# Eighteen of a layer's 22 tail gates by seven products a pair, in a two-layer decoder trunk

## The chip, the cores and the metric

The kernel runs on one core of one Trainium2 chip. The metric is device time in microseconds (us); lower is better. Matmuls run on TensorE (PE; its weight loads are listed apart as PEld), elementwise work on VectorE (DVE), ScalarE (ACT) and GpSimd (POOL), and DMAs are issued by SyncE (its queue is SPq). Each engine works through its instructions in a fixed order: one that waits holds up all that stand behind it on that engine, and this holds for the DMA issues of SyncE too.

## What is computed

Two layers, each of four token mixers whose results are merged under sigmoid gates (cut from the reference):

```
h = rms_norm(x, norm_g)
z = h @ w_in                    # 1024 tokens, 1024 channels; the last 4096 columns are merge_logits
...
gates = sigmoid(merge_logits + b_merge).reshape(bsz, seq, 4, 1024)
merged = (gates[:, :, 0] * (y_a @ w_br_a) + gates[:, :, 1] * (y_b @ w_br_b)
          + gates[:, :, 2] * (y_c @ w_br_c) + gates[:, :, 3] * (y_m @ w_br_m))
x = x + merged @ w_out
```

The kernel calls the branches i = 0, 1, 2, 3 (a, b, c, m) and cuts each branch's gate into 8 blocks c of 128 channels, so a layer has 32 gates (i, c). A gate is a 1024x1024 by 1024x128 product, a scale per token, and a tanh.

## The kernel before

Everything is kept with channels on the 128 partitions and the 1024 tokens along the row. For precision every operand is split into a high part in fp32r and a low part (`xh`, `xl`, `wh`, `wl`), and a product is the three matmuls high by high, low by high, high by low (`block_into`). A 128x1024 result takes two matmuls of 512 columns for each; one gate (8 blocks of input channels) is 48 matmuls, and a branch's projection `y @ w_br` for one c is 12 matmuls (24 for i = 1).

`wsplit` loads a weight tile (`wr`, two buffers), casts it on DVE (`wh`) and subtracts on POOL (`wl`). `cmn` multiplies the product by `rsb`, the per-token scale, on DVE, out of PSUM. The PSUM tiles of these products, `mm`, have two buffers of 128x1024. A Tile scheduler decides each engine's order from the order of the code and from priorities, and it puts in the waits; the buffers of the pools (38 row tiles from `U`, two each of `wr`, `wh`, `wl`) decide when a load may start.

Ten gates of a layer (the list `BG`: all of i = 1, and (3, 6) and (3, 7)) are made earlier, by `background`, and stored in DRAM as `bgscr`. The other 22 are made in the tail of the layer, after `branch_a`: `merge` runs for i = 0, 2, 3, 1, and for each c makes the gate with `cmn` and a tanh on ACT, then the projection `psy`, then `(1 + gate) * psy` on DVE (L103), and adds it to `merged` on POOL. For a gate of `BG` it loads the tile `gate` from `bgscr` in place of the product. `gated` fetches the branch outputs from DRAM (`ysscr`) while the merge before is running. After the merges come eight blocks of the output projection `w_out`.

Of the kernel before, what the change touches and what calls it, by code (L numbers as in the profile page):

```python
# [35 lines left out]
BR_OFF = (0, 2, 6, 8)  # L36
# [8 lines left out]
class Trunk:  # L45
# [174 lines left out]
    def setup(self):  # L220
        nc, a, L = self.nc, self.a, self.L
        C = self.C
        self.ident = C([P, P], "ident")
        make_identity(nc, self.ident)
        self.identb = C([P, P], "identb", BF16)
        make_identity(nc, self.identb)
        self.ones = C([P, 1], "ones")
        nc.vector.memset(self.ones, 1.0)
        self.onesr = C([P, P], "onesr", F32R)
        nc.vector.tensor_copy(self.onesr, self.ones.to_broadcast([P, P]))  # L230
        self.maskb = C([P, P], "maskb", BF16)
# [34 lines left out]
        self.bgscr = self.dp.tile([len(BG), P, S], F32, name="bgscr")  # L266
# [1019 lines left out]
    def bg_gate(self, l, br, b):  # L1286
        bi = {1: B_BG, 2: B_CG, 3: B_MG}[br] + b
        y = {1: self.ybscr, 2: self.gscr, 3: self.ymscr}[br][b]
        ri = {1: 0, 2: 0, 3: 4}[br] + b
        self.background(l, bi, y=y, ri=self.riscr[ri], dst=self.ysscr[BR_OFF[br] - 2 + b])  # L1290

    def bg_merge(self, l, i, c):
        at = l * 32 + 8 * i + c
        self.background(l, B_MRG + 8 * i + c, bias=self.bm_half[:, at:at + 1], dst=self.bgscr[BG.index((i, c))])

    def gated(self, br, own):

        ys = []
        for b in range(BR_KT[br]):
            pair = None  # L1300
            if b < min(own, 2):
                pair = self.wpair(True)
            elif b < own:
                pair = [self.fp.tile([P, S], F32R, tag="ft", name=self._n("ys")) if 2 * b + k < 7 else self.U("ys", F32R)
                        for k in range(2)]
            ys.append(self.fetch(self.ysscr[BR_OFF[br] - 2 + b], pair, self.wraw(True), self.nc.vector))
        return ys

    def silu2(self, l, bi):
# [94 lines left out]
            ya.append((hi, lo))  # L1404
        return ya

    def merge(self, l, i, ys, first=False, last=False, ahead=None):

        nc = self.nc
        kt = BR_KT[i]  # L1410
# [2 lines left out]
            self.mg = []  # L1413
        if last:
            self.mgs = []
        res = None

        def weights(c):
            off = (BR_OFF[i] * 8 + c * kt) * P
# [2 lines left out]

        nxt = weights(0)
        for c in range(8):
            if ahead and ahead[0] == c:
                res = ahead[1]()
# [23 lines left out]
        return res  # L1450

    def run(self):
        nc, a = self.nc, self.a
# [16 lines left out]
        for l in range(self.L):  # L1470
# [69 lines left out]


NU = 38
AH = (6, 4, 3)
NBW = 2
LOW = 100000

# [120 lines left out]
```

## Time and profile before

| | |
|---|---|
| time, median of 3 runs (lowest to highest) | 2438.87 us (2436.58 to 2439.66) |
| the profiled execution's own time | 2440.25 us |
| its span, first to last instruction | 2438.5 us |
| mean granted TensorE clock | 0.988 |
| PE busy | 2325.2 us, 95% of the span |
| PEld busy | 1855.2 us, 76% |
| DVE / POOL / ACT busy | 1215.9 / 775.0 / 706.5 us |
| HBM traffic | 97 GB/s over the span |

The busy times are sums over the whole program; PE and PEld run side by side. The tails with which this case deals lie at about 809 to 1130 us (layer 0) and 2104 to 2355 us (layer 1), and the output projections follow.

### The profile page before, as it was taken

The page shows a single profiled execution, that of the slowest core. Times are in us where ns is not written, and L with a number is a line of the kernel's source. Part 1 is how long each engine was busy: PE and PEld are TensorE (multiplying, and loading weights), DVE is VectorE, ACT ScalarE, POOL GpSimd, SP SyncE. Part 2 cuts the span into 40 slices and gives each one's busy share as a digit, 9 for nine tenths or more (in the row PEclk, how much of TensorE's full clock was granted, in tenths as well). Part 3 has the DMA queues.
Part 4 walks back from the last instruction along what each step waited for, and adds up shares of the span by engine and source line. Part 5 has one row for each costly group of instructions (what it writes and reads, how often), then busy time and mean ns, then how long its engine had stood idle before and what let it go on. Part 6 is the DMA issues. An engine that isn't in the chain of part 4 may idle for free. (4 is left out here: it accounts for less than half of the span.)

```text
span 2438.5 us, 28178 instructions
## 1 busy us (share of the span) xinstructions
PE 2325.2 (95%) x11174; PEld 1855.2 (76%) x11174; DVE 1215.9 (50%) x1871; ACT 706.5 (29%) x1233; POOL 775.0 (32%) x605
## 2 busy tenths in 40 slices
PE   7998889989999999999999888999999999999999
PEld 5766677867778888888877666787777888888887
DVE  6455784366676323236244556714666652233351
ACT  4121253247762101101111213522577420111010
POOL 3533113432304214342435421143322132244411
PEclk9999999999999999999999999999999999999999
DMA  4226343242332112222432363413423211122342
GB/s 153 75 93 184 115 138 102 82 123 79 95 106 66 61 44 70 69 77 105 156 100 73 96 188 108 139 49 103 125 83 109 80 44 52 56 92 79 103 156 69
DMA packets 91700, 237.56 MB, mean 97 GB/s; under 512 B 25200, under 2 KB 34352, under 8 KB 91568
## 3 DMA queue, kind: packets, MB, share of 16 engines
q1 hardware_dynamic: 91568, 235.76, 30.4%
q8 instruction: 88, 1.44, 0.2%
q14 instruction: 44, 0.36, 0.1%
HBM read 175.27 MB, written 60.46 MB: 97 GB/s over the span
## 5 line engine op out<-in xcount | busy, mean ns | idle before, releaser
L96 POOL TENSOR_TENSOR wl<-wr,wh 128x1024 fp32r<-128x1024 f32 (+3 forms) x125 | 295.9, 2367 | 946.1 <-DVE wh L152 634.7
L176 PE MATMUL mm<-xh,wh 128*128 128x512 f32 x1216 | 378.7, 392 | 9.1 <-ACT xh L106 8.7
L152 DVE CAST wh<-wr 128x1024 fp32r<-128x1024 f32 (+2 forms) x110 | 78.4, 713 | 618.6 <-PE mm L176 539.8
L176 PE MATMUL mm<-xh,wl 128*128 128x512 f32 x1216 | 376.1, 390 | 0.8 <-POOL wl L96 0.8
L176 PE MATMUL mm<-xl,wh 128*128 128x512 f32 x1216 | 376.8, 390 | 0.0
L176 PEld LDWEIGHTS mm<-xh,wh 128*128 128x128 f32 x1216 | 227.3, 188 | 59.9 <-ACT xh L106 8.7
L176 PEld LDWEIGHTS mm<-xh,wl 128*128 128x128 f32 x1216 | 228.3, 188 | 49.7 <-POOL wl L96 1.6
L176 PEld LDWEIGHTS mm<-xl,wh 128*128 128x128 f32 x1216 | 228.4, 188 | 49.0 <-issue 0.8
L176 PE MATMUL bg<-xh,bh 128*128 128x512 f32 x576 | 229.2, 416 | 15.5 <-DVE bgx L96 15.5
L176 PE MATMUL bg<-xl,bh 128*128 128x512 f32 x576 | 226.3, 411 | 0.0
L176 PE MATMUL bg<-xh,bl 128*128 128x512 f32 x576 | 224.1, 409 | 1.0 <-POOL bl L96 1.0
L96 POOL TENSOR_TENSOR bl<-br,bh 128x1024 fp32r<-128x1024 f32 x36 | 96.4, 2678 | 317.0 <-DVE bh L152 203.3
L106 ACT ACTIVATE cmn<-cmn,bmh 128x1024 f32<-128x1024 f32 x44 | 50.6, 1151 | 440.7 <-DVE cmn L96 440.7
L96 DVE TENSOR_TENSOR pT<-tr,pT 128x512 fp32r<-128x512 f32 x224 | 125.6, 571 | 42.8 <-ACT pT L106 42.1
L176 PEld LDWEIGHTS bg<-xh,bh 128*128 128x128 f32 x576 | 111.8, 195 | 46.0 <-DVE bgx L96 25.6
L176 PE MATMUL pv<-pT,v 128*128 128x512 f32 (+3 forms) x384 | 134.0, 388 | 7.9 <-DVE pT L96 5.1
L106 ACT ACTIVATE pT<-tr 128x512 fp32r<-128x512 f32 x224 | 111.0, 505 | 86.6 <-PE tr L1087 77.3
L176 PEld LDWEIGHTS bg<-xh,bl 128*128 128x128 f32 x576 | 111.1, 193 | 24.9 <-issue 3.2
L1054 DVE TENSOR_REDUCE mx<-mm 128x1 f32<-128x128 f32 (+7 forms) x128 | 96.5, 754 | 64.5 <-PE mm L176 63.7
L176 PEld LDWEIGHTS bg<-xl,bh 128*128 128x128 f32 x576 | 111.3, 194 | 21.8 <-issue 4.0
L106 ACT ACTIVATE pr<-mm,nm,qs 128x128 f32<-128x128 f32 (+7 forms) x128 | 106.3, 830 | 0.9
L1087 PE MATMUL tr<-ident,pr 128*128 128x128 f32 x576 | 97.9, 275 | 0.3 <-ACT pr L106 0.2
(449 smaller groups left out, 4173.7 us busy)
## 6 DMA issues: line engine op xcount, KB each, us to landing
wr<-in_w_cm_dram SPq DMA_DIRECT2D x76, 512.0 KB, 3.6
br<-in_w_cm_dram SPq DMA_DIRECT2D x36, 512.0 KB, 3.7
bgscr<-bgx SPq DMA_DIRECT2D x20, 512.0 KB, 3.1
gate<-bgscr SPq DMA_DIRECT2D x20, 512.0 KB, 5.6
ysscr<-bgx SPq DMA_DIRECT2D x16, 512.0 KB, 2.6
br<-ysscr SPq DMA_DIRECT2D x16, 512.0 KB, 3.4
wr<-in_w_out_dram SPq DMA_DIRECT2D x16, 512.0 KB, 3.7
bgr<-riscr SPq DMA_DIRECT2D x24, 256.0 KB, 4.8
```

The lines of the kernel that those rows point to most:

```text
L96: (eng or self.nc.vector).tensor_tensor(out=out, in0=x, in1=y, op=op)
L106: self.nc.scalar.activation(out, x, f, **k)
L152: self.nc.vector.tensor_copy(hi[:, :n], raw)
L176: self.nc.tensor.matmul(out, lhsT, rhs, start=start, stop=stop)
L1054: nc.vector.reduce_max(out=mx, in_=ps[:, 0:n], axis=AX.X)
L1087: nc.tensor.transpose(pt[:, k * P:(k + 1) * P], pts[k][:, st * P:(st + 1) * P], self.ident)
```

## The change

In `after` no gate is made inside `merge` any more. All 32 are stored in `bgscr` first, and `merge` loads each as a `gate` tile. The 22 tail gates are made ahead of the merges:

- Four, (0, 0) to (0, 3), in the ordinary way (`gate`: `cmn`, tanh, a store).
- Eighteen as nine pairs (i, c), (i, c + 1) by Strassen's scheme in its seven-product form: the weights of the two gates are the two rows of a 2x2 block matrix, the input channels are cut into halves (blocks k and k + 4), and the tokens into halves of 512. Each of the seven products has 4 blocks by 3 matmuls, so a pair takes 84 matmuls of 512 columns in place of 96. `pair_weights` forms the four sums of weights (DVE, tiles `sa`), and splits seven 128x512 weights (`sw`: high part on ACT, low part on POOL, two of the seven on DVE). `pairs` adds the products up on DVE (tiles `us`; the results go to `wh` and `wl` tiles), POOL multiplies by `rsb`, ACT takes the tanh, each on 512 columns, and SyncE stores the halves.
- The sums of x that the products need (`T` and `T4`, and later `xl`/`xh` written over) come from `x_sums`, for k = 0 to 3: it loads blocks k and k + 4 of x again (`xp`), scales them on ACT, forms four sums on POOL (`tp`, `t1`, in place), and splits three of them (ACT copy, DVE subtraction). The code interleaves these with the four ordinary gates. `x_sums2` then splits the fourth sum over half of `xg`.

Two smaller edits come with it. `gated` fetches through `U("yr")` in place of the `br` tile, all of them in the first two merges. The additions to `merged` alternate between POOL (odd c) and DVE. The last attention gate's `background` gets ordinary priority (`fore`).

```diff
+    def x_sums(self, l, src, k):
+        g, v = self.nc.gpsimd, self.nc.vector
...
+        b11, b12, b21, b22 = self.x_part(src, l, k)
+        t = self.U("tp")
+        t3, t2 = t[:, 0:512], t[:, 512:1024]
+        self.tt(t3, b22, b12, SUB, eng=g)
+        self.tt(t2, t3, b11, ADD, eng=g)
+        self.tt(self.t1[k // 2][:, k % 2 * 512:k % 2 * 512 + 512], b12, b11, SUB, eng=g)
+        self.tt(b21, b21, t2, SUB, eng=g)
+        self.split(*self.T[3][k], t3)
+        self.split(*self.T[2][k], t2)
+        self.split(*self.T[4][k], b21)
+    def pair_weights(self, aps):
+        raw = [self.wraw() for _ in range(2)]
...
+        self.tt(s1, a21, a22, ADD)
+        self.tt(s2, s1, a11, SUB)
+        self.tt(s3, a11, a21, SUB)
+        self.tt(s4, a12, s2, SUB)
+        for i, a in enumerate((a11, s2, s3, a12, s1, a22, s4)):
+            w = self.U("sw", F32R)
+            hi, lo = half(w)
+            self.split(hi, lo, a, sub_eng=self.nc.vector if i in (1, 4) else self.nc.gpsimd)
+            yield hi, lo
+    def pairs(self, todo):
...
+            q1, q2 = half(self.mm())
+            self.act(u1, prod(q1, 11), AF.Copy)
+            self.tt(u2, prod(q2, 2), u1, ADD)
+            q1, q2 = half(self.mm())
+            self.tt(u3, prod(q1, 3), u2, ADD)
+            finish(0, c1[0], prod(q2, 21), u1)
+            q1, q2 = half(self.mm())
+            p5 = prod(q1, 1)
+            self.tt(u4, p5, u2, ADD)
+            finish(1, c2[1], p5, u3)
+            finish(0, c2[0], prod(q2, 4), u3)
+            finish(1, c1[1], prod(self.pv(), 22), u4)
+            done(c1, c2)
+    def gate(self, l, i, c):
+        g, b = self.cmn(l, B_MRG + 8 * i + c), l * 32 + 8 * i + c
+        self.act(g, g, AF.Tanh, scale=0.5, bias=self.bm_half[:, b:b + 1])
+        self.nc.sync.dma_start(out=self.bgscr[8 * i + c], in_=g)
...
-            if (i, c) in BG:
-                g = self.U("gate")
-                nc.sync.dma_start(out=g, in_=self.bgscr[BG.index((i, c))])
-            else:
-                g = self.cmn(l, B_MRG + 8 * i + c)
-                self.act(g, g, AF.Tanh, scale=0.5, bias=self.bm_half[:, l * 32 + 8 * i + c:l * 32 + 8 * i + c + 1])
+            g = self.U("gate")
+            nc.sync.dma_start(out=g, in_=self.bgscr[8 * i + c])
...
-                self.tt(self.mg[c], self.mg[c], g, ADD, eng=None if last else nc.gpsimd)
+                self.tt(self.mg[c], self.mg[c], g, ADD, eng=nc.gpsimd if c % 2 and not last else None)
...
             ysa = self.branch_a(l)
-            ys = self.merge(l, 0, ysa, first=True, ahead=(AH[0], lambda: self.gated(2, 2)))
-            ys = self.merge(l, 2, ys, ahead=(AH[1], lambda: self.gated(3, 0)))
-            ys = self.merge(l, 3, ys, ahead=(AH[2], lambda: self.gated(1, 4)))
-            self.merge(l, 1, ys, last=True)
+            for k in range(4):
+                self.x_sums(l, src, k)
+                if k:
+                    self.gate(l, 0, k - 1)
+            self.gate(l, 0, 3)
+            self.x_sums2()
+            todo = [(i, c) for i in (0, 2, 3, 1) for c in range(8) if (i, c) not in BG][4:]
+            self.gate_pairs(l, todo[::2])
...
+            self.merge(l, 0, ysa, first=True, ahead={0: lambda: get(2, 0), 4: lambda: get(3, 0)})
+            self.merge(l, 2, ys[2], ahead={0: lambda: get(1, 4)})
+            self.merge(l, 3, ys[3])
+            self.merge(l, 1, ys[1], last=True)
```

**Where the instructions stand.** DVE in the tail of layer 0, before, from the end of `branch_a` on (`cmn_...<-mm_...,rsb` reads a gate's product out of PSUM, `merged` is the gated projection, a `wh` or `wkh` cast is the high part of the next weights):

```order
L96 TENSOR_TENSOR yal_1333_6772<-cmn_1308_6597,yah_1332_6771 128x1024
L152 CAST wkh_1335_6777<-wr_1334_6775 128x1024
L96 TENSOR_TENSOR wkl_1336_6778<-wr_1334_6775,wkh_1335_6777 128x1024
L96 TENSOR_TENSOR cmn_1337_6781<-mm_1341_6788,rsb_89_557 128x1024
L103 SCALAR_TENSOR_TENSOR merged0_1343_6852<-cmn_1337_6781,mm_1342_6839 128x1024
L152 CAST wh_1356_6936<-wr_1355_6934 128x1024
L152 CAST wh_1363_7009<-wr_1362_7007 128x1024
L96 TENSOR_TENSOR cmn_1344_6854<-mm_1348_6861,rsb_89_557 128x1024
```

The same place in `after` (`mm_1358`, `mm_1366`, `mm_1374`, `mm_1379` are the products of the four ordinary gates in this order; `tp_1350`, `tp_1353`, `tp_1361` and the `xp` tiles belong to k = 0, 1, 2):

```order
L96 TENSOR_TENSOR T4_1344_6785<-xp_1349_6792,T4_1342_6783 128x512
L152 CAST wh_1377_7037<-wr_1376_7035 128x1024
L96 TENSOR_TENSOR cmn_1354_6823<-mm_1358_6830,rsb_89_557 128x1024
L96 TENSOR_TENSOR T_1340_6781<-tp_1353_6812,T_1338_6779 128x512
L96 TENSOR_TENSOR T_1336_6777<-tp_1353_6812,T_1334_6775 128x512
L96 TENSOR_TENSOR T4_1344_6785<-xp_1352_6809,T4_1342_6783 128x512
L96 TENSOR_TENSOR T_1341_6782<-tp_1361_6888,T_1339_6780 128x512
L96 TENSOR_TENSOR T_1337_6778<-tp_1361_6888,T_1335_6776 128x512
L96 TENSOR_TENSOR T4_1345_6786<-xp_1360_6885,T4_1343_6784 128x512
L96 TENSOR_TENSOR cmn_1362_6899<-mm_1366_6906,rsb_89_557 128x1024
```

Between the reads of the first and the second product now stand the six subtractions of k = 1 and k = 2; and the cast of the fourth gate's weights, `wh_1377`, stands ahead of the read of the first product. In the order the cast takes the `wh` buffer that the second gate's matmuls read.

SyncE at the same place in `after` (in `before` its queue holds weight loads alone here):

```order
L1415 DMA xp_1352_6809<-in_xT_dram 128x1024
L1455 DMA wr_1381_7102<-in_w_cm_dram 128x1024
L1415 DMA xp_1359_6882<-in_xT_dram 128x1024
L1510 DMA bgscr_248<-cmn_1354_6823 128x1024
L1415 DMA xp_1360_6885<-in_xT_dram 128x1024
L1415 DMA xp_1367_6958<-in_xT_dram 128x1024
L1415 DMA xp_1368_6961<-in_xT_dram 128x1024
L1510 DMA bgscr_248<-cmn_1362_6899 128x1024
```

The store of the first gate, `cmn_1354`, stands ahead of the load of the second x block of k = 2, `xp_1360`.

SyncE around the start of the merges in `after` (`wh_1545` and `wl_1546` hold the last pair's gates, `gate_1560`, `gate_1563`, `gate_1569`, `gate_1572`, `gate_1581` are the tiles for c = 0, 1, 2, 3, 4 of i = 0; `wr_1612` is a tile of w_br):

```order
L1552 DMA gate_1560_8406<-bgscr_248 128x1024
L1524 DMA bgscr_248<-wh_1545_8278 128x512
L1524 DMA bgscr_248<-wl_1546_8279 128x512
L1552 DMA gate_1563_8423<-bgscr_248 128x1024
L1552 DMA gate_1569_8446<-bgscr_248 128x1024
L149 DMA wr_1612_8624<-in_w_br_dram 128x1024
L1552 DMA gate_1572_8463<-bgscr_248 128x1024
L1019 DMA yr_1575_8480<-ysscr_249 128x1024
L1019 DMA yr_1578_8486<-ysscr_249 128x1024
L1552 DMA gate_1581_8492<-bgscr_248 128x1024
L1552 DMA gate_1584_8509<-bgscr_248 128x1024
```

The gates that the first merge reads are loaded behind the stores of the last pair, and that of c = 3 behind a weight load. The same happens once more a merge later:

```order
L1019 DMA yr_1604_8580<-ysscr_249 128x1024
L1019 DMA yr_1607_8586<-ysscr_249 128x1024
L149 DMA wr_1627_8732<-in_w_br_dram 128x1024
L1552 DMA gate_1608_8590<-bgscr_248 128x1024
L1552 DMA gate_1610_8607<-bgscr_248 128x1024
```

Here `gate_1608` is that of c = 0 of i = 2, and stands behind `wr_1627`, whose buffer comes free when POOL has read the weight tile before it in that buffer. In `before` gate loads stand on this queue in merge i = 1 alone:

```order
L149 DMA wr_1573_8854<-in_w_out_dram 128x1024
L149 DMA wr_1581_8920<-in_w_out_dram 128x1024
L1433 DMA gate_1516_8465<-bgscr_248 128x1024
L1433 DMA gate_1518_8482<-bgscr_248 128x1024
L149 DMA wr_1589_8986<-in_w_out_dram 128x1024
L149 DMA br_1523_8505<-in_w_br_dram 128x1024
L1433 DMA gate_1526_8511<-bgscr_248 128x1024
```

The order is the same in both layers. Over the program PE has 216 matmuls fewer (12 for each of 18 pairs). The largest new groups on the other engines are 126 sums out of PSUM and 72 weight sums on DVE, 126 splits of `sw` and 72 tanh on ACT, and 90 subtractions for `sw` and 72 multiplications by `rsb` on POOL, all of 512 columns; 44 gate loads and 80 stores come to SyncE.

## Rows read from the trace of the kernel before

**Rows 1.** The page: busy time by engine, and the granted clock in 40 slices.

```profile
PE 2325.2 (95%) x11174; PEld 1855.2 (76%) x11174; DVE 1215.9 (50%) x1871; ACT 706.5 (29%) x1233; POOL 775.0 (32%) x605
...
PEclk9999999999999999999999999999999999999999
```

**Rows 2.** Windows: stretch, busy time of each engine, granted clock, DMA share, GB/s.

```profile
core 0: us, PE busy (x) PEld busy (x) DVE busy (x) ACT busy (x) POOL busy (x), PEclk, DMA share, GB/s
960.00:980.00 20.00, 20.00 (x90) 16.57 (x89) 4.99 (x5) 2.21 (x2) 7.19 (x3) 1.00 0.31 101
1120.00:1140.00 20.00, 19.62 (x85) 15.37 (x84) 14.37 (x11) 3.18 (x3) 3.08 (x2) 1.00 0.49 184
2125.00:2136.00 11.00, 9.94 (x41) 7.27 (x40) 8.90 (x9) 3.05 (x3) 6.29 (x3) 1.00 0.42 142
```

**Rows 3.** One tile's instructions, cmn, 925 to 960 us: DVE's reads of gate products.

```profile
L96 DVE TENSOR_TENSOR cmn<-mm,rsb x3: 1217/1217/1218, 928.7 to 955.9; 128x1024 f32<-128x1024 f32 x3
```

**Rows 4.** Timeline, 998 to 1002 us: last matmuls of a product, and who reads it.

```profile
998.54 0.61 PE L176 MATMUL mm<-bh,wkl 128*128 128x512 f32 x2
...
999.26 1.22 DVE L103 SCALAR_TENSOR_TENSOR cmn<-cmn,mm 128x1024 f32<-128x1024 f32 x1 [1.36 <-PE mm L176]
```

**Rows 5.** Groups by line, engine, operation and shape: count, busy us, mean ns.

```profile
L96 POOL TENSOR_TENSOR wl<-wr,wh 128x1024 fp32r<-128x1024 f32 x95 | 231.8, 2440 | 798.2 <-DVE wh L152 594.4 <-PE mm L176 188.6 <-DVE fi L96 12.0
...
L96 DVE TENSOR_TENSOR pT<-tr,pT 128x512 fp32r<-128x512 f32 x128 | 85.8, 685 | 28.1 <-ACT pT L106 27.5
...
L106 ACT ACTIVATE pT<-tr 128x512 fp32r<-128x512 f32 x128 | 74.5, 598 | 45.1 <-PE tr L1087 36.1 <-PE tr L1155 8.3
...
L152 DVE CAST wh<-wr 128x1024 fp32r<-128x1024 f32 x96 | 70.9, 738 | 555.9 <-PE mm L176 487.6 <-issue 52.6 <-DMA wr<-in_w_cm_dram 12.6
...
L96 DVE TENSOR_TENSOR cmn<-mm,rsb 128x1024 f32<-128x1024 f32 x52 | 63.3, 1217 | 0.0
L106 ACT ACTIVATE cmn<-cmn,bmh 128x1024 f32<-128x1024 f32 x44 | 50.6, 1151 | 440.7 <-DVE cmn L96 440.7
...
L96 POOL TENSOR_TENSOR v<-wr,v 128x512 fp32r<-128x512 f32 x16 | 20.6, 1289 | 0.0
...
L106 ACT ACTIVATE v<-wr 128x512 fp32r<-128x512 f32 x16 | 10.0, 624 | 0.1
...
L106 ACT ACTIVATE xh<-xres,consts 128x1024 fp32r<-128x1024 f32 x8 | 9.2, 1154 | 67.6 <-DVE xres L96 50.0 <-issue 17.6
```

**Rows 6.** The page: DMA issues, KB each, median us from issue to landing.

```profile
wr<-in_w_cm_dram SPq DMA_DIRECT2D x76, 512.0 KB, 3.6
...
gate<-bgscr SPq DMA_DIRECT2D x20, 512.0 KB, 5.6
```

**Rows 7.** Waits of SyncE's DMA queue, 1060 to 1130 us: total us, times, longest.

```profile
SPq L149 <- POOL wkl L96: 17.8, 3, 9.3
```

**Rows 8.** Timeline of SyncE's queue in the same stretch.

```profile
1097.62 0.33 SPq L149 DMA_DIRECT2D br<-in_w_br_dram  x1
1098.00 0.43 SPq L1433 DMA_DIRECT2D gate<-bgscr  x1
```

**Rows 9.** Timeline, 1126 to 1130 us: a late gate, and PE behind it.

```profile
1126.05 1.22 DVE L103 SCALAR_TENSOR_TENSOR gate<-gate,mm 128x1024 f32<-128x1024 f32 x1 [1.88 <-DMA gate<-bgscr]
...
1127.32 0.74 PE L176 MATMUL mm<-bh,wkh 128*128 128x512 f32 x2 [0.33 <-DVE gate L103]
```

**Rows 10.** Window 1126 to 1131 us, columns as in rows 2.

```profile
1126.00:1131.00 5.00, 4.67 (x21) 3.51 (x20) 3.73 (x4) 1.06 (x1) 0.00 (x0) 1.00 1.03 417
```

**Rows 11.** One tile's instructions, merged, whole run: duration ns, min/median/max.

```profile
L96 DVE TENSOR_TENSOR merged<-merged,gate x16: 1224/1226/2401, 1106.6 to 2351.8; 128x1024 f32<-128x1024 f32 x16
```

**Rows 12.** Timeline, 1104 to 1112 us: POOL's subtraction and DVE's addition beside it.

```profile
1105.07 2.41 POOL L96 TENSOR_TENSOR wkl<-br,wkh 128x1024 fp32r<-128x1024 f32 x1
1106.58 1.97 DVE L96 TENSOR_TENSOR merged<-merged,gate 128x1024 f32<-128x1024 f32 x1
```

More of the change, by code (lines that the diff above doesn't have):

```diff
@@ L1305, in gated @@
                         for k in range(2)]
-            ys.append(self.fetch(self.ysscr[BR_OFF[br] - 2 + b], pair, self.wraw(True), self.nc.vector))
+            ys.append(self.fetch(self.ysscr[BR_OFF[br] - 2 + b], pair, self.U("yr"), self.nc.vector))
         return ys
@@ L1405, in branch_a, with x_part @@
         return ya
-    def merge(self, l, i, ys, first=False, last=False, ahead=None):
+    def x_part(self, src, l, k):
+        res = []
+        for j in (k, k + 4):
+            x = self.U("xp")
+            self.nc.sync.dma_start(out=x, in_=src[j])
+            self.act(x, x, AF.Identity, scale=self.norm_g[:, l * 8 + j:l * 8 + j + 1])
+            res += [x[:, 0:512], x[:, 512:1024]]
+        return res
+    def x_sums(self, l, src, k):
+        g, v = self.nc.gpsimd, self.nc.vector
+        at = lambda t, j: [x[j // 2][:, j % 2 * 512:j % 2 * 512 + 512] for x in t]
+        if k == 0:
+            b = lambda tag: self.bp.tile([P, 1024], F32R, tag=tag, name=self._n("T"), **({"bufs": 1} if tag == "br" else {}))
+            f = lambda: self.fp.tile([P, S], F32R, tag="ft", name=self._n("T"))
+            t2, t3 = ([b("bh"), b("bh")], [b("bl"), b("bl")]), ([f(), f()], [f(), b("br")])
+            t4 = [[self.U("T4", F32R) for _ in range(2)] for _ in range(2)]
+            self.T = {i: [at(t, j) for j in range(4)] for i, t in ((2, t2), (3, t3), (4, t4))}
+            self.t1 = [self.U("t1") for _ in range(2)]
+        b11, b12, b21, b22 = self.x_part(src, l, k)
[8 more added lines that the diff above has]
+        self.split(*self.T[4][k], b21)
@@ new lines, in x_sums2 @@
+    def x_sums2(self):
+        half = lambda k, h: [x[:, h * 512:h * 512 + 512] for x in self.xg[k]]
+        self.T[1] = [half(k, 1) for k in range(4)]
+        self.T[11] = [half(k, 0) for k in range(4)]
+        self.T[21], self.T[22] = [[half(k + 4, h) for k in range(4)] for h in range(2)]
+        for k in range(4):
+            self.split(*self.T[1][k], self.t1[k // 2][:, k % 2 * 512:k % 2 * 512 + 512])
+    def pair_weights(self, aps):
+        raw = [self.wraw() for _ in range(2)]
+        for x, ap in zip(raw, aps):
+            self.nc.sync.dma_start(out=x, in_=ap)
+        half = lambda t: (t[:, 0:512], t[:, 512:1024])
+        (a11, a12), (a21, a22) = half(raw[0]), half(raw[1])
+        (s1, s2), (s3, s4) = half(self.U("sa")), half(self.U("sa"))
+        self.tt(s1, a21, a22, ADD)
[7 more added lines that the diff above has]
+            yield hi, lo
@@ new lines, in pairs, with prod @@
+    def pairs(self, todo):
+        half = lambda t: (t[:, 0:512], t[:, 512:1024])
+        nxt = self.pair_weights(todo[0][0])
+        ws = [next(nxt) for _ in range(7)]
+        for n, (_, finish, done) in enumerate(todo):
+            nxt = self.pair_weights(todo[n + 1][0]) if n + 1 < len(todo) else None
+            nws = []
+            def prod(ps, x):
+                hi, lo = ws[len(nws)]
+                for k in range(4):
+                    xh, xl = self.T[x][k]
+                    sl = slice(k * P, (k + 1) * P)
+                    self.mmr(ps, hi[:, sl], xh, k == 0, False)
+                    self.mmr(ps, hi[:, sl], xl, False, False)
+                    self.mmr(ps, lo[:, sl], xh, False, k == 3)
+                nws.append(next(nxt) if nxt else None)
+                return ps
+            (u1, u2), (u3, u4) = half(self.U("us")), half(self.U("us"))
+            c1, c2 = [half(t.bitcast(F32)) for t in self.wpair()]
+            q1, q2 = half(self.mm())
[11 more added lines that the diff above has]
+            done(c1, c2)
+            ws = nws
@@ new lines, in gate, with gate_pairs, finish, done @@
+    def gate(self, l, i, c):
+        g, b = self.cmn(l, B_MRG + 8 * i + c), l * 32 + 8 * i + c
+        self.act(g, g, AF.Tanh, scale=0.5, bias=self.bm_half[:, b:b + 1])
+        self.nc.sync.dma_start(out=self.bgscr[8 * i + c], in_=g)
+    def gate_pairs(self, l, pairs):
+        def finish(h, out, x, y):
+            self.tt(out, x, y, ADD)
+            self.tt(out, out, self.rsb[:, h * 512:h * 512 + 512], MUL, eng=self.nc.gpsimd)
+        def done(at):
+            def f(*cs):
+                for k, c in enumerate(cs):
+                    b = l * 32 + at + k
+                    for h in range(2):
+                        self.act(c[h], c[h], AF.Tanh, scale=0.5, bias=self.bm_half[:, b:b + 1])
+                        self.nc.sync.dma_start(out=self.bgscr[at + k][:, h * 512:h * 512 + 512], in_=c[h])
+            return f
+        self.pairs([([self.a["w_cm"][l, B_MRG + 8 * i + c + k] for k in range(2)], finish, done(8 * i + c)) for i, c in pairs])
@@ L1409, in merge @@
+    def merge(self, l, i, ys, first=False, last=False, ahead={}):
         nc = self.nc
@@ L1424, in merge @@
         for c in range(8):
-            if ahead and ahead[0] == c:
-                res = ahead[1]()
+            if c in ahead:
+                ahead[c]()
             if c % per == 0:
@@ L1517, in run, with get @@
             ysa = self.branch_a(l)
-            ys = self.merge(l, 0, ysa, first=True, ahead=(AH[0], lambda: self.gated(2, 2)))
-            ys = self.merge(l, 2, ys, ahead=(AH[1], lambda: self.gated(3, 0)))
-            ys = self.merge(l, 3, ys, ahead=(AH[2], lambda: self.gated(1, 4)))
-            self.merge(l, 1, ys, last=True)
+            for k in range(4):
+                self.x_sums(l, src, k)
[5 more added lines that the diff above has]
+            self.gate_pairs(l, todo[::2])
+            ys = {0: ysa}
+            def get(i, own):
+                ys[i] = self.gated(i, own)
+            self.merge(l, 0, ysa, first=True, ahead={0: lambda: get(2, 0), 4: lambda: get(3, 0)})
+            self.merge(l, 2, ys[2], ahead={0: lambda: get(1, 4)})
+            self.merge(l, 3, ys[3])
+            self.merge(l, 1, ys[1], last=True)
             for c in range(8):
```

15 lines of the change are left out of this document (6 added, 9 removed).

## The prediction, made before the changed kernel ran

> **What bounds the kernel now.** I read the page's busy times first. PE is busy 95% of the span, every other engine half or less, and the granted clock is 0.9 or more in all 40 slices, the upper of its two levels (2.4 GHz) [rows 1]. An average over the program says little about the tail, so the windows came next. In the merges i = 0, 2, 3 the reader sees PE busy 20.00 of 20 us: nothing waits there, and a matmul removed is time removed. Only merge i = 1, which already loads its gates, loses something: 0.38 us of 20 in layer 0, and 1.06 of 11 us at its entry in layer 1 [rows 2]. The step of a matmul comes from DVE's reads of gate products: from the first to the third are 27.2 us, so 13.6 us for a gate and a projection, 48 + 12 matmuls, 0.2267 us each [rows 3]. From the start of a product's last matmul to its reader on DVE are 0.49 us, since the second of the two in the row starts 0.23 us after 998.54 [rows 4].
>
> **What is removed.** 12 matmuls for each of 9 pairs: 108 x 0.2267 = 24.5 us a layer, all of it on the path.
>
> **What is added** is work for DVE, ACT, POOL and SyncE, on engines with room. So the question is not how much it is but which PE instruction ends up behind it. I followed the order at four places. Prices [rows 5]: a cast 0.74, a weight subtraction on POOL 2.44, a 512-wide POOL operation 1.29, a 512-wide DVE operation 0.69, an ACT copy of 512 columns 0.60 to 0.62, a read of a gate product 1.22, a tanh or a scale of 1024 columns 1.15. The new sums differ from these rows in operands only, so I take them as they stand. A load of 512 KB takes 3.6 us to land, a gate load 5.6 [rows 6].
>
> First place, the four ordinary gates. PSUM holds two products, so the fourth needs DVE's read of the second, and ahead of that read stand the splits of k = 2. Their chain starts when the second gate's last matmul with `wh` begins, for which `wh_1377` waits: reaction 0.49, cast 0.74, POOL `wl` 2.44, two sums of k = 1 on POOL 2.58, their ACT copy 0.60, the tanh of the first gate 1.15. Only now may SyncE issue that gate's store (0.4), and behind it stands the load of `xp_1360`, 3.6 to land. Then the scale 1.15, four POOL sums 5.16, ACT copy 0.60, DVE 0.69, and the read 1.22: 20.8 us. Undisturbed, PE would begin the fourth gate 51 matmuls after the same instant, 11.6 us. Loss 9.3 us; about 8 if every POOL sum is somewhat shorter, 11 if store and load slow each other. Nothing else is in PE's order to cover it. The wait of the third gate on the first product (2.4 us of chain behind the same cast) lies inside this.
>
> Second place, the first product. Its weights' high part stands on ACT behind the fourth gate's tanh: 0.49 + 1.22 + 1.15 + 0.62 + POOL 1.29 = 4.8 us until its third matmul, which would come after 0.7. Loss 4.1. The other weights of this pair leave POOL at 1.29 each against 2.7 us of PE a product, which holds, but the next pair's raw tiles wait for these; I add 1.4. Sum 5.5, bounds 4 to 7.
>
> Third place, the steady pairs. Weights are made half a pair or more ahead, and a pair's 19.0 us of PE cover some 11 us of POOL, 9 of DVE and 7 of ACT. What PE does wait for is the emptying of PSUM tiles in mid-pair. Three times it has 4, 4 and 7 matmuls as cover (0.91, 0.91, 1.59 us), against a reaction and an ACT copy, a reaction and one DVE sum, a reaction and two DVE sums: 1.1, 1.2, 1.9. That is 0.7 us a pair at most, 6.3 for nine; some wait may be covered already by the one before it, so I take 4.5, with 0 as the lower end.
>
> Fourth place, the merges. Each c now has only 12 matmuls, 2.72 us, in place of 13.6, so all that hid behind the gate products is bare. SyncE's order makes the gates late. The last pair's last half leaves PE, then DVE, POOL, ACT: 0.49 + 0.69 + 1.29 + 0.60 = 3.1 us. Its two stores stand ahead of the gate of c = 1, issued at 3.9 and landed at 9.5. Then DVE's product 1.22, the cast of the next `w_br` 0.74 and POOL's 2.44, for the weight load `wr_1612` waits until POOL has read that buffer: 13.9. Behind it the gate of c = 3, landed at 19.9, and with DVE's 1.22 PE begins c = 5 at 21.1 instead of 13.6. A landing at the short end would give 6 us, and the two DVE subtractions of fetched branch outputs ahead of c = 4 hold it to about 8.5. In the next merge it happens again: cast 0.74, POOL 2.44, issue 0.4, landing 5.6, DVE 1.22 = 10.4 us from DVE's last product of i = 0, where PE alone would want the buffer after 3.7. Loss 6 with some queueing taken off. Merge i = 3 has its loads issued early and i = 1 has 5.4 us a c; I see nothing late there. Sum 14.5, bounds 9 to 19.
>
> The trace of before shows this mechanism in small: SyncE waits three times for POOL's `wkl`, up to 9.3 us; the gate load stands right behind the weight load and goes only after it (1097.62, 1098.00) [rows 7, 8]. A late gate then holds PE: DVE idles 1.88 us on a gate's DMA, and PE starts 0.05 us after DVE is done [rows 9]. Several 512 KB loads at once go at 417 GB/s, 1.26 us each [rows 10], so a burst is not the limit; the order is.
>
> **The sum.** A layer: -24.5 + 9.3 + 5.5 + 4.5 + 14.5 = +9.3. Two layers +18.6, less the 1.0 us that layer 1 now loses at its entry to i = 1. The profiled execution's own time is 2440.25 us, 1.75 over its span and 1.4 over the median; 2440.25 + 17.6 - 1.4 = 2456.5, so I forecast 2457. All lower ends together give -3.5 a layer and 2431, all upper ends +18.8 and 2475.
>
> **The rivals.** *Everything hides* (5%). PE is the full engine, the others have half their time free, and the order could leave the new work beside PE: -49 us, 2390. For it speaks the 20.00 of 20 us [rows 2]; against it that PE's own cover is what shrinks. The Trainium skill, "Perfetto Trace Analysis", section "Identifying the Most-Contended Engine", says to improve the engine with the highest occupancy first, and to judge TensorE by its weight loads rather than its matmuls. By that rule, with PEld at 76% and above all others here, this is the outcome to expect; the trace agrees on which engine it is, and no row can say whether the rest stays hidden.
>
> *One of the two large losses does not come about* (15%). The mechanism is the distance between an issue and a landing: if gate loads or x loads go a few microseconds earlier, because the U tiles and queue slots they wait for are free early and POOL keeps ahead, either chain drops out. Without the first two places a layer is -24.5 + 4.5 + 14.5 = -5.5, without the fourth -24.5 + 19.3 = -5.2: both 2427, faster. The point at which it decides is 19 us of new waits a layer beside the 4.5 in the pairs; the sum above has 29.
>
> *No change* (9%): both chains at their lower ends, 2434 to 2444.
>
> *Worse* (13%): DVE and POOL hinder each other. The addition to `merged` on DVE, both inputs in SBUF, mostly takes 1.23 us but up to 2.40 [rows 11]; one of 1.97 us began beside a POOL subtraction that still had 0.9 us to run [rows 12]. A pair now has six such DVE sums against nine POOL operations. If one of the three waits in a pair meets one, 1.29 x 9 = 11.6 us a layer more, 23 in all: 2480. The Trainium skill, "SBUF — State Buffer", section "SBUF: two separate sides", says that such a DVE operation and a GpSimd one hold a shared port pair in turn, each for its whole duration; the spread from 1.23 to 2.40 agrees. Against it: the sums that PE waits for read PSUM.
>
> **How the numbers follow.** The forecast has 58%. About 0.2% (5 us) is what a measurement of this kernel can tell from no change. Slower: the forecast and the worse case, 0.71 or so; faster: the first two rivals, 0.20; between them 0.09. The range must take in most of the "one loss" case's upper side and the contention: 2430 to 2480; for the forecast alone it is 2446 to 2470.
>
> **What would show it.** In the changed kernel's trace: PE idle of some 9 us before the fourth gate's product, released by DVE's read of the second; some 4 us at the first product, released by ACT; about half a microsecond a pair; in merge i = 0 and at the start of i = 2 idle of 14 us in sum, released by DVE's product, which itself waits for a gate's DMA; SyncE waiting for POOL's `wkl` with gate loads behind it. Windows with PE at 20 of 20 there, or gates landing before PE is done with the pairs, would prove me wrong.

## The result: 69 us slower, and the profile after

The median is 2507.2 us (2504.18 to 2510.96, 4 runs) against 2438.07 us of the kernel before, a ratio of 1.0288 (95% interval 1.0273 to 1.0302). The direction was forecast; the size was not: 2457 was predicted with an upper end of 2480.

The page of the changed kernel, the lines that answer to [rows 1] and [rows 6] (`yr` takes the place of `br<-ysscr`):

```profile
PE 2313.8 (92%) x10958; PEld 1829.5 (73%) x10958; DVE 1403.0 (56%) x2081; ACT 836.4 (33%) x1461; POOL 915.5 (37%) x747
...
PEclk9999999999999899989999999999999998999999
...
gate<-bgscr SPq DMA_DIRECT2D x64, 512.0 KB, 7.2
...
yr<-ysscr SPq DMA_DIRECT2D x16, 512.0 KB, 8.3
```

PE has 216 matmuls less, but only 11 us less busy time in a span that is 67 us longer: 216 at 0.2267 us would be 49, so what is left has become slower. The clock now dips below 90% in three slices, all of which touch the tails, and a gate load lands after 7.2 us in place of 5.6.

Windows of the changed kernel over the tail of layer 0, columns as in [rows 2]. The stages are the four ordinary gates, the nine pairs, and the merges i = 0, 2, 3, 1, each up to the first matmul of the next:

```profile
801.72:853.74 52.02, 36.99 (x153) 29.55 (x152) 24.82 (x26) 23.51 (x29) 26.59 (x18) 0.90 0.32 111
853.74:1047.87 194.13, 179.80 (x756) 142.24 (x757) 96.49 (x117) 65.86 (x106) 106.95 (x80) 0.98 0.32 108
1047.87:1082.07 34.20, 26.08 (x98) 19.91 (x96) 16.27 (x15) 8.88 (x9) 4.85 (x4) 0.90 0.68 252
1082.07:1108.59 26.52, 24.65 (x97) 19.86 (x98) 23.11 (x18) 0.00 (x0) 15.67 (x7) 0.87 0.85 323
1108.59:1135.76 27.17, 24.65 (x98) 18.89 (x97) 25.84 (x17) 0.00 (x0) 23.48 (x9) 0.94 0.45 155
1135.76:1179.22 43.46, 43.46 (x194) 35.99 (x192) 30.40 (x24) 6.75 (x7) 7.67 (x4) 1.00 0.31 118
```

A stage's time less its matmuls at 0.2267 us [rows 3] is what it loses. By the order the stages have 151, 756, 96, 96, 96 and 192 matmuls (a window counts those that overlap it, one or two more). The losses are 17.8, 22.7, 12.4, 4.7, 5.4 and 0.0 us: 63 in a layer. Layer 1 gives 17.9, 23.1, 12.1, 4.7, 5.2, 0.0. From the end of `branch_a` to the output projection the tail takes 377.5 us in both layers, against 340.8 and 344.3 before (803.5 to 1144.3 us and 2003.4 to 2347.7 us there; the tail of layer 1 begins some 100 us ahead of the 2104 given with the profile of before): +36.7 and +33.2, and everything else together is 3 us shorter.

PE's waits in the three parts of that tail (total us, times, longest):

```profile
PE mm L176 <- DVE cmn L96: 11.8, 2, 10.3
...
PE mm L176 <- ACT us L106: 9.9, 6, 1.7
PE mm L176 <- ACT sw L106: 3.2, 1, 3.2
PE mm L176 <- DVE wl L96: 2.6, 1, 2.6
...
PE mm L176 <- DVE merged L103: 6.1, 3, 2.2
PE mm L176 <- DVE gate L103: 2.4, 2, 2.1
PE mm L176 <- DVE wkh L152: 2.0, 1, 2.0
PE mm L176 <- POOL wkl L96: 1.9, 1, 1.9
```

The long wait for `cmn`, those for `sw` and those for `merged` (all three in i = 0) were forecast. Those of the last three lines were not forecast as they stand: `gate` is waited for in i = 3, and at the start of i = 2 PE waits for the weights themselves, `wkh` and `wkl`. Nor was `wl` (2.6 us, in the second pair). The largest that was not is `us` on ACT: the copy of a pair's first product. That copy stood in the forecast, but not a wait of 1.6 us a pair for it. The timeline of one pair shows where it stands:

```profile
903.67 0.72 ACT L106 ACTIVATE wl<-wl,bmh 128x512 f32<-128x512 f32 x1 [4.81 <-POOL wl L96]
904.92 0.72 ACT L106 ACTIVATE wh<-wh,bmh 128x512 f32<-128x512 f32 x1 [0.53 <-POOL wh L96]
905.55 0.58 ACT L106 ACTIVATE us<-mm 128x512 f32<-128x512 f32 x1
...
906.18 4.83 PE L176 MATMUL mm<-T,sw 128*128 128x512 f32 x20 [1.64 <-ACT us L106]
```

Two tanhs of the pair before stand ahead of the copy, and they wait for POOL's multiplications, which wait for that pair's last sums. The last matmul of the product had begun at 903.24, so it was ready at some 903.7.

The clock is seen behind the fourth gate's wait. Two matmuls there take 1.06 us where they took 0.61, a step of 0.43 in place of 0.227, the lower of the two levels:

```profile
826.66 0.61 PE L176 MATMUL mm<-xh,wl 128*128 128x512 f32 x2
837.53 1.22 PE L176 MATMUL mm<-xh,wh 128*128 128x512 f32 x2 [10.26 <-DVE cmn L96]
838.55 1.06 PE L176 MATMUL mm<-xl,wh 128*128 128x512 f32 x2
839.40 1.06 PE L176 MATMUL mm<-xh,wl 128*128 128x512 f32 x2
...
841.70 0.63 PE L176 MATMUL mm<-xh,wl 128*128 128x512 f32 x2
```

Counted over the tail of layer 0, 51 recorded matmuls have this step, in seven groups of 6 to 11, each behind a wait of some 2 us or more (1.8 to 10.3) or a cluster of them: 51 x 0.20 = 10 us a layer. In the whole run there are some 200, before some 100. Not every such wait has its group: behind one of 2.2 us at 1067.89 in i = 0 the matmuls go on at 0.23, and so they do behind a longer one outside the tails:

```profile
1426.88 0.50 PE L176 MATMUL tr<-wh,kvh 128*128 128x512 f32 x1 [3.26 <-DVE vt L100]
```

### The profile page after: what moved, and what is told of

The parts are those of the page before. It is cut to its first block, busy times and chain, and to the rows that moved or that the text cites. A ratio compares the mean times of both kernels' runs of the same rounds, so it can differ in the third digit from the quotient of the medians.

```text
span 2505.7 us, 28737 instructions
## 1 busy us (share of the span) xinstructions
PE 2313.8 (92%) x10958; PEld 1829.5 (73%) x10958; DVE 1403.0 (56%) x2081; ACT 836.4 (33%) x1461; POOL 915.5 (37%) x747
## 5 line engine op out<-in xcount | busy, mean ns | idle before, releaser
L96 POOL TENSOR_TENSOR wl<-wr,wh 128x1024 fp32r<-128x1024 f32 (+3 forms) x89 | 213.9, 2403 | 616.6 <-DVE wh L152 354.5
L176 PE MATMUL mm<-xh,wh 128*128 128x512 f32 x640 | 203.7, 398 | 30.4 <-DVE cmn L96 22.0
L176 PE MATMUL mm<-xl,wh 128*128 128x512 f32 x640 | 201.5, 395 | 0.0
L176 PE MATMUL mm<-xh,wl 128*128 128x512 f32 x640 | 200.0, 393 | 0.7 <-POOL wl L96 0.7
L176 PE MATMUL mm<-T,sw 128*128 128x512 f32 x648 | 162.4, 401 | 24.9 <-ACT us L106 19.8
L176 PEld LDWEIGHTS mm<-T,sw 128*128 128x128 f32 x648 | 121.3, 191 | 60.1 <-ACT us L106 25.4
L176 PEld LDWEIGHTS mm<-xh,wh 128*128 128x128 f32 x640 | 120.5, 191 | 59.7 <-DVE cmn L96 18.8
L176 PE MATMUL mm<-xh,sw 128*128 128x512 f32 x432 | 144.4, 402 | 10.3 <-ACT sw L106 6.4
L176 PEld LDWEIGHTS mm<-xl,wh 128*128 128x128 f32 x640 | 121.7, 190 | 27.0 <-issue 0.8
L176 PEld LDWEIGHTS mm<-xh,wl 128*128 128x128 f32 x640 | 121.3, 190 | 27.3 <-POOL wl L96 1.6
```

Source lines behind the costliest of these rows:

```text
L96: (eng or self.nc.vector).tensor_tensor(out=out, in0=x, in1=y, op=op)
L176: self.nc.tensor.matmul(out, lhsT, rhs, start=start, stop=stop)
```

## The experiments

Stage losses in layer 0 as above (us), and the medians. The kernel before ran beside each, at 2435 to 2441 us; the ratios are to those runs.

| run | median | gates | pairs | i = 0 | i = 2 | i = 3 | i = 1 |
|---|---|---|---|---|---|---|---|
| changed kernel | 2507.2 | 17.8 | 22.7 | 12.4 | 4.7 | 5.4 | 0.0 |
| e1_dvecopy | 2486.1 | 16.9 | 14.5 | 10.5 | 4.5 | 5.4 | 0.0 |
| e2_actstore | 2492.8 | 15.5 | 23.7 | 8.7 | 4.9 | 5.2 | 0.0 |
| e14_two | 2474.9 | 14.3 | 15.6 | 7.2 | 4.5 | 5.4 | 0.0 |
| e5_nopairs | 2481.4 | 2.4 | none | 11.8 | 4.4 | 5.2 | 0.0 |
| e4_dve | 2504.0 | 18.0 | 22.6 | 10.8 | 5.0 | 5.1 | 0.0 |
| e4_pool | 2508.2 | 17.6 | 22.8 | 10.1 | 4.4 | 8.0 | 0.0 |
| e10_noadd | 2493.2 | 16.9 | 22.3 | 11.4 | 4.4 | 0.0 | 0.0 |
| e3_wbr_u | 2504.1 | 17.8 | 22.6 | 13.3 | 6.3 | 1.5 | 1.7 |
| e13_uw | 2575.3 | 14.1 | 15.4 | 6.9 | 6.0 | 1.5 | 7.7 |

**The copy moved to DVE.**

```diff
-            self.act(u1, prod(q1, 11), AF.Copy)
+            self.nc.vector.tensor_copy(u1, prod(q1, 11))
```

> The copy of a pair's first product out of PSUM is made by DVE and no longer by ACT. Theory (order): in the changed kernel PE waits for this copy 9.9 us a layer because it stands on ACT behind tanhs of the pair before; on DVE nothing late stands ahead of it, so most of 2 x 9.9 us comes back: 2487 (2483 to 2492), and a steady pair takes about 19.8 us in place of 21.3. Rival (throughput): the pairs are set by the sum of new work on DVE, ACT and POOL, and 0.69 us more on DVE a pair changes nothing or costs: 2505 to 2515.

Measured 2486.1 us, ratio to before 1.0208 (1.0191 to 1.0225). The copies on DVE in this run:

```profile
903.04 0.69 DVE L1492 COPY us<-mm 128x512 f32<-128x512 f32 x1 [0.80 <-PE mm L176]
...
922.57 0.69 DVE L1492 COPY us<-mm 128x512 f32<-128x512 f32 x1 [0.80 <-PE mm L176]
```

The copies of two pairs in a row are 19.53 us apart; in the changed kernel the first DVE sums of two pairs in a row were 21.31 apart:

```profile
909.23 0.69 DVE L96 TENSOR_TENSOR us<-mm,us 128x512 f32<-128x512 f32 x1 [1.86 <-PE mm L176]
...
930.54 0.69 DVE L96 TENSOR_TENSOR us<-mm,us 128x512 f32<-128x512 f32 x1 [1.90 <-PE mm L176]
```

A steady pair now loses 0.5 us over its 84 matmuls, the price that the forecast had for it. The throughput rival falls: DVE has more to do than before and the pair is faster. PE's instructions stand in the same order in both runs.

**The stores taken off SyncE.**

```diff
-        self.nc.sync.dma_start(out=self.bgscr[8 * i + c], in_=g)
+        self.nc.scalar.dma_start(out=self.bgscr[8 * i + c], in_=g)
...
-                        self.nc.sync.dma_start(out=self.bgscr[at + k][:, h * 512:h * 512 + 512], in_=c[h])
+                        self.nc.scalar.dma_start(out=self.bgscr[at + k][:, h * 512:h * 512 + 512], in_=c[h])
```

> The stores of the gates made in the tail are issued from ACT's queue, so that no load on SyncE stands behind a store. Theory (head of the queue): the second x block of k = 2 is issued 3.9 us earlier, and the first merge's gate loads no longer wait for the last pair's tanh: the long wait before the fourth gate falls from 10.3 us to some 6.5, merge i = 0 loses some 4 us less a layer, 2507 - 16 = 2491; the issues cost ACT some 0.3 us each, of which a part comes back as a longer wait in the pairs: 2488 to 2500. Rival: POOL's chain alone sets the fourth gate, and the weight loads behind POOL set the merges: within 3 us of 2507, or slower by ACT's issues.

Measured 2492.8, ratio 1.0235 (1.0220 to 1.0250). In the changed kernel the load of `xp_1360` went only at 823.24, behind the store:

```profile
822.87 0.33 SPq L1510 DMA_DIRECT2D bgscr<-cmn  x1
823.24 1.79 SPq L1415 DMA_DIRECT2D xp<-in_xT_dram  x3
...
828.24 1.15 ACT L106 ACTIVATE xp<-xp,consts 128x1024 f32<-128x1024 f32 x1 [3.52 <-DMA xp<-in_xT_dram]
...
836.26 1.22 DVE L96 TENSOR_TENSOR cmn<-mm,rsb 128x1024 f32<-128x1024 f32 x1
```

Here it goes right behind its neighbour, and PE's longest wait for `cmn` is shorter:

```profile
PE mm L176 <- DVE cmn L96: 9.0, 2, 7.5
```

The wait falls from 10.3 to 7.5 us, not to 6.5: the rest of the chain, on POOL, stays. Merge i = 0 loses 3.7 less; the issues cost the pairs 1.0.

**Both together.**

> The copy on DVE and the stores from ACT's queue together; the base for the run beside it. If the two losses are separate: 2507 - 21 - 14 = 2472 (2468 to 2477), with merge i = 0 losing some 9 us a layer as with the stores alone.

Measured 2474.9, ratio 1.0156 (1.0139 to 1.0173). The two add up: taken against the runs of before beside them, the gains are 20 and 13 us alone and 32 together.

**No pairs.** The 22 gates are made by `gate` one after the other, and `x_sums`, `x_sums2` and `gate_pairs` are not called.

> All 22 gates are made in the ordinary way ahead of the merges, without x sums and without pairs; the merges stay as in the changed kernel. The work of TensorE is that of the kernel before. Theory: the merges lose some 22 us a layer by themselves, since nothing is left in them that covers DVE, POOL and loads: 2438 + 2 x 22 - 5 = 2477 (2468 to 2485). Rival: the loss in the merges comes from what the pairs leave behind (late sums, late stores), and then most of it is gone: 2440 to 2455.

Measured 2481.4, ratio 1.0185 (1.0168 to 1.0203). With TensorE's work as before, taking the gates out of the merges costs some 43 us: 11.8 + 4.4 + 5.2 a layer in the merges, nearly as with the pairs. So 49 us saved in matmuls stood against 43 us that the merges lost by themselves, before any cost of the pairs.

**Who adds to merged.** All by DVE, or all but those of i = 1 by POOL:

```diff
-                self.tt(self.mg[c], self.mg[c], g, ADD, eng=nc.gpsimd if c % 2 and not last else None)
+                self.tt(self.mg[c], self.mg[c], g, ADD, eng=None)
```

> All additions to merged are made by DVE (in the changed kernel every second one by POOL). In merge i = 3 of the changed kernel DVE is busy 19 of 20 us, and its additions take up to 3.4 us beside POOL's. Theory (DVE and POOL in each other's way): with POOL left with the weight subtractions alone an addition on DVE takes 1.2 us, DVE has 1.22 + 1.23 + 0.37 for a c of 2.72 us, and i = 3 loses some 2 us in place of 5.3: 2500 (2497 to 2503). Rival (i = 2 and i = 3 wait for loads, or DVE's own sum is the limit): 2505 to 2512.

> All additions to merged but those of i = 1 are made by POOL, as in the kernel before. Theory (DVE and POOL in each other's way): DVE's products read PSUM and are not held, so i = 2 and i = 3 stop losing to DVE; but POOL needs 2.4 + 1.2 us for a c of 2.72 and falls some 14 us behind, which gate tiles that come free late and i = 1 pay: 2507 to 2520. Rival (the merges wait for loads alone): 2504 to 2510, and no new wait for POOL in PE's table.

Measured 2504.0 (1.0276, 1.0253 to 1.0299) and 2508.2 (1.0303, 1.0281 to 1.0326). The first lies between the two ranges given for it, the second in both of its own, and in neither run did i = 3 come out as the theory had it. The additions in the changed kernel, and in the run with all on DVE:

```profile
L96 DVE TENSOR_TENSOR merged<-merged,gate x32: 1224/1793/3418, 1091.9 to 2417.9; 128x1024 f32<-128x1024 f32 x32
```

```profile
L96 DVE TENSOR_TENSOR merged<-merged,gate x48: 1210/1226/2553, 1091.2 to 2421.2; 128x1024 f32<-128x1024 f32 x48
...
1100.00:1120.00 20.00, 18.43 (x79) 14.22 (x78) 19.86 (x17) 0.00 (x0) 7.33 (x4) 1.00 0.65 251
```

The median addition falls from 1.79 to 1.23 us with POOL's additions gone, which is what the hindrance would do; but with twice the additions in i = 2 and i = 3 DVE is busy 19.86 of 20 us, and the loss stays at 5.1. With all on POOL that engine is busy in all 29.8 us of i = 3, which loses 8.0.

**No additions.** A line `if last:` stands ahead of the addition.

> Leaves out the additions to merged in i = 2 and i = 3 (those of i = 0 are assignments, i = 1 still adds). Theory (DVE and POOL set i = 2 and i = 3): these lose some 4 us in sum in place of 10, i = 0 stays: 2495 (2491 to 2500). Rival (they wait for loads): 2503 to 2509.

Measured 2493.2, ratio 1.0240 (1.0225 to 1.0255). The window of i = 3:

```profile
1105.06:1126.82 21.76, 21.76 (x97) 18.02 (x96) 11.89 (x11) 0.00 (x0) 9.60 (x4) 1.00 0.69 249
```

PE is busy in all of it, with every gate load still there, so without the additions i = 3 loses nothing. In i = 2 they matter little (4.4 for 4.7). The additions are needed for this loss but are not all of it: in e3_wbr_u and e13_uw below they are all there, and i = 3 loses 1.5. In e3_wbr_u that is no gain, since i = 0, i = 2 and i = 1 lose more, and the four merges together lose 22.8 us for 22.5; a backlog on DVE and POOL that is paid in one merge or in another would look so, but this was not tested apart.

**The loads of the merges.** Four runs asked whether the gate loads come late by their place on SyncE.

```diff
-                               raw=self.wraw(last),
+                               raw=self.U("wb"),
```

> The branch weights of the merges are loaded into U tiles of their own in place of the two wr buffers (br in the last merge), so that no gate load stands behind a weight load that waits for POOL. Theory (head of the queue): the loss of 10.3 us in i = 0 falls to about 5 and the start of i = 2 loses 2 to 3 us less: 2507 - 2 x 7 = 2493 (2487 to 2498). Rival (DVE and POOL in each other's way): DVE is busy 17 to 19 of 20 us from i = 2 on, so what is gained in i = 0 is lost behind it: over 2502.

> Leaves out the 32 gate loads of a layer: the merges multiply by the tile rsb in place of the gates. Everything else stays. Theory (late gate loads set merge i = 0; DVE and POOL set i = 2 and i = 3): i = 0 loses some 3 us in place of 12, the other two 4 to 5 as before: 2489 (2484 to 2494). Rival (loads, by order or bandwidth, set all three merges): all of the 22 us fall to 4 or less: 2471.

> Leaves out both, the gate loads and the additions of i = 2 and i = 3. Theory (two separate causes): what each gave adds up, some 2477. If the merges still lose over 10 us a layer then, it is the branch outputs and weights that arrive late, or the projections' own readers on DVE: over 2485.

Measured 2504.1 (1.0280, 1.0263 to 1.0296), 2523.7 (1.0366, 1.0349 to 1.0384) and 2504.6 (1.0287, 1.0272 to 1.0303). In e3_wbr_u the freed `wr` buffers went to loads of `w_out`, and one of those, waiting for POOL, now stood ahead of the gate of c = 1. In e9_noload the scheduler put the casts and subtractions of the branch weights elsewhere, and PE waited 15 us for these; in e11_neither it waited 8.5 us for them, and the second outcome that was named for that run (over 2485, weights that arrive late) came. Neither says anything on the gate loads. Next the gate loads went to ACT's queue, on top of e1_dvecopy:

> On top of the copy on DVE (2486), the gate loads of the merges are issued from ACT's queue, so that none of them stands behind a weight load on SyncE that waits for POOL; the stores and the weight loads keep their order and their buffers. Theory (order on SyncE): i = 0 loses 6 in place of 10.5 us a layer and i = 2 some 1.5 less: 2474 (2469 to 2480). Rival (weights behind DVE and POOL, or the bandwidth of the loads, hold i = 0 and i = 2 as much): 2483 to 2490.

Measured 2526.0 (1.0356, 1.0325 to 1.0387), 40 us slower than its base (36 when each is taken against the runs of before beside it). ACT's queue shows why:

```profile
1056.93 1.06 ACT L106 ACTIVATE fh<-yr 128x1024 fp32r<-128x1024 f32 x1 [14.02 <-DMA yr<-ysscr]
1058.19 1.06 ACT L106 ACTIVATE fh<-yr 128x1024 fp32r<-128x1024 f32 x1 [0.20 <-DMA yr<-ysscr]
1058.27 2.44 ACTq L1552 DMA_DIRECT2D gate<-bgscr  x4
```

Four gate loads stand behind copies that wait 14 us for fetched outputs, which themselves stand behind a weight load on SyncE. Here the place in the queue decided, on ACT as it does on SyncE. The last run takes every load that waits for POOL off SyncE's way, with `w_out` in U tiles too, on top of e14_two:

> On top of that the raw weights of the merges and of the output projection both come into U tiles, so that no load on SyncE around the merges has to wait for POOL to read one of the two wr buffers. Theory (order on SyncE sets merge i = 0 and the start of i = 2): i = 0 loses 4 to 5 us in place of 9, i = 2 some 3 in place of 5: 2460 (2455 to 2465). Rival (bandwidth of the loads, or DVE's cast and POOL's subtraction of the branch weights): i = 0 stays at 8 or more with the DMA share near 1, or PE waits for wkh and wkl: 2468 or more.

Measured 2575.3 (1.0564, 1.0542 to 1.0586). The output projections lose some 50 us a layer, since their weights now come too late. But up to i = 3 the run bears on the question: the loads of the first two gates of i = 0 are issued at 1029.00, 7 us ahead of the merge's first matmul (in the changed kernel the first of them went 0.6 us ahead), and PE's waits in i = 0 and i = 2 are

```profile
PE mm L176 <- POOL wkl L96: 3.0, 2, 1.8
PE mm L176 <- DVE merged L103: 2.8, 1, 2.8
PE mm L176 <- DVE wkh L152: 2.0, 1, 2.0
```

i = 0 still loses 6.9 us (7.2 in its base). Gate loads are not what holds it then: DVE's product stands behind a subtraction that waits for ACT, which is still at the tanhs of the last pair, and at the entry to i = 2 PE waits for the cast and the subtraction of the weights, as in the changed kernel.

**A wait filled with work.** 40 matmuls that nobody reads, ahead of `self.gate(l, 0, 3)`, so between the third and the fourth of the four gates, where the long wait is (the expectation names the second and the third):

```diff
+            ps = self.tr()
+            for j in range(40):
+                self.mmr(ps, self.xg[4][0][:, 0:P], self.xg[4][0][:, 0:512], j == 0, j == 39)
             self.gate(l, 0, 3)
```

> 40 matmuls whose result nobody reads are put on PE between the second and the third ordinary gate of each layer, 9.1 us that PE would otherwise wait before the fourth. Theory (the fall of the granted clock has a price of its own beside the wait): the wait shrinks to about 1 us, the chain that ends it is as long as before, and the eight matmuls at half speed behind the wait, 1.6 us a layer, go at full speed: 2504 (2502 to 2506). Rival (the fall of the clock is only another name for the wait): 2507, and half-speed matmuls behind the fourth gate's start as before.

Measured 2504.7, ratio 1.0284 (1.0265 to 1.0304): in the theory's range, and not to be told from 1.0288. What decides is the trace. The wait shrank from 10.3 to 2.1 us, and the half-speed matmuls behind it are still there:

```profile
835.19 0.73 PE L176 MATMUL mm<-xh,wh 128*128 128x512 f32 x2 [2.10 <-DVE cmn L96]
836.34 1.05 PE L176 MATMUL mm<-xh,wl 128*128 128x512 f32 x2
```

So the price of the clock was not removed, and the number does not confirm the theory. What the run shows is that this wait of 2.1 us is followed by as many slow matmuls (7) as the one of 10.3.

**Three gains at once:** copy, stores, and all additions on DVE.

> The copy on DVE, the stores from ACT's queue and all additions on DVE together. If the three losses are separate, their gains add up: 2507 - 21 - 14 - 7 = 2465 (2460 to 2472). If they hide each other, 2472 to 2485.

Measured 2473.1 (1.0153, 1.0129 to 1.0176), not to be told from e14_two: the additions give nothing on top. No version came below the kernel before.

## Why the prediction was wrong, point by point

**Removed work:** right. 12 matmuls a pair, 24.5 us a layer. What went wrong is what was added: 33.8 us of new losses were forecast for a layer, and 63 were measured.

**First and second place (gates, first product):** the mechanism was right, link by link: the cast, POOL, tanh, store, load, POOL, the read. Sized at 13.4 us, measured 17.8. The load landed in 5.0 us (823.24 to 828.24) in place of 3.6, POOL made one more sum ahead of the weight subtraction, and about 1.4 us are the slower clock.

**Third place (pairs):** this is the step that failed. I wrote that PE waits for "a reaction and an ACT copy", 1.1 us against a cover of 0.91. That priced the copy and not what stands ahead of it on ACT: two tanhs that end behind POOL's multiplications of the pair before. A steady pair lost 2.3 us and not 0.5, and e1_dvecopy, which moves only this copy, brings 0.5 and some 20 us in all. The stage was sized at 5.9 us (the 1.4 of the second pair's tiles and 4.5) and lost 22.7. Six steady pairs have 13.5 of these, and the first two 4.2 and 4.7, for which the forecast had little over 2 together; this second shortfall, weights and sums that are late in turn, no run took away (in e1_dvecopy the first two pairs lose 11.1 of the 14.5 that remain).

**Fourth place (merges):** sized at 14.5 us, measured 22.5: i = 0 at 8.5 and 12.4, i = 2 at 6 and 4.7, i = 3 at nothing and 5.4. SyncE's order was as forecast, and it is seen in the changed kernel:

```profile
1051.41 0.63 SPq L1524 DMA_DIRECT2D bgscr<-wl  x1
1052.14 0.92 SPq L1552 DMA_DIRECT2D gate<-bgscr  x2
1061.41 0.33 SPq L149 DMA_DIRECT2D wr<-in_w_br_dram  x1
1061.84 0.38 SPq L1552 DMA_DIRECT2D gate<-bgscr  x1
```

Its price was only partly right: the stores ahead of the gates are worth 3.7 us in i = 0 (e2_actstore), but with the gates early most of the rest stays (e13_uw). In i = 2 the size came near by luck. The forecast had PE wait for DVE's product and this for a gate's DMA; PE waited for the cast and for POOL's subtraction themselves (`wkh` 2.0, `wkl` 1.9 us), and 11 slow matmuls followed. "I see nothing late there" of i = 3 was wrong: 5.4 us, and none without the additions on DVE and POOL (e10_noadd). The rival that named this hindrance had it in the pairs. The Trainium skill, "SBUF — State Buffer", section "SBUF: two separate sides", has DVE operations with two SBUF inputs and GpSimd operations take turns at one port pair; the additions' median of 1.79 us beside POOL's (POOL busy 23.48 of 27.17 us in i = 3) and 1.23 without them (13.27 of 26.90) agree.

**No term at all** stood for the clock. 51 half-speed matmuls in layer 0 are 10 us. They lie inside the losses of the stages above and cannot be added to them: of the 29 us a layer by which these exceed the forecast, 17 are in the pairs (11 of them the copy in six steady pairs), 8 in the merges and 4 in the gates. The clock's share is a count; no run took it away, with the waits or without them.

**Layer 1's wait before:** I credited 1.0 us, as a loss at the entry to i = 1. The window of [rows 2] from 2125 to 2136 us lies elsewhere: merge i = 1 of layer 1 began at 2303, and at 2125 the tail was in i = 2, where gates are still made, as the matmul behind one of the three short waits shows.

```profile
2134.29 0.73 PE L176 MATMUL mm<-xh,wh 128*128 128x512 f32 x2 [0.31 <-DVE cmn L103]
```

So the prediction's "nothing waits there", read in layer 0, does not hold for all of i = 0, 2 and 3. The credit was also too small: the tail of layer 1 was 3.5 us longer than that of layer 0 before (1.6 of these are seven matmuls of background work inside it), and this is gone. (The prediction's point of decision, "19 us of new waits", should be 20: 24.5 - 4.5. Nothing hangs on it.)

**The chances:** slower had 0.71, and slower came, for reasons that were in part others. The rival in which everything hides fell with the first wait; e5_nopairs shows that the merges pay some 43 us even with no pair and no sum of x. The worse case named DVE and POOL in the pairs and gave 2480; a steady pair without the late copy loses no more than was forecast (e1_dvecopy), so the pairs do not show it.

What stays open is how the 7 us in i = 0 and the 4.7 in i = 2 divide between DVE, POOL and the clock; no run removed them.

## What to carry to other kernels

For each instruction that PE waits for, price not only the instruction but what stands ahead of it on its own engine, down to what that in turn waits for; one copy on an engine that was busy 33% of the span cost 20 us here. Taking matmuls out of a stage also takes away cover, the work of PE behind which that of the other engines hides: before counting what is saved, ask what the remaining matmuls must still hide, and run that stage without the saving (e5_nopairs) to see the bill. And look behind each new wait of PE for slow matmuls: in these tails most waits of some 2 us or more had them, a second price that the waits do not show.

## What the runs showed of the hardware

In the tail of layer 0 matmuls went at the lower clock behind PE waits of 2.1 us (e7_fill) as behind those of 10.3 (the changed kernel): 6 to 11 of them took 0.43 us in place of 0.227, about 1.4 us a time. Behind the 1.6 us waits of the steady pairs they did not, and in the changed kernel neither behind two longer ones (2.2 us at 1067.89, 3.3 us at 1426.88). A DVE addition of two SBUF tiles took up to 3.4 us in the merges, where the shortest took 1.22. DVE's products in the same merges, with one input in PSUM, were never lengthened:

```profile
L103 DVE SCALAR_TENSOR_TENSOR gate<-gate,mm x48: 1204/1214/1222, 1090.6 to 2416.7; 128x1024 f32<-128x1024 f32 x48
```

A 512 KB load of a gate or a branch output took 7.2 or 8.3 us to land (medians over the run); while i = 0 and i = 2 ran, 252 and 323 GB/s were moving. A load of gate weights took 3.7, and over the whole span the mean was 117 GB/s.
